# Banded attention's value product on 64-column stationary tiles, three products in the same rows of PSUM

## The chip, the cores and the metric

The kernel runs on one core of one Trainium2 chip. The metric is the device time of one launch in microseconds (us), lower is better. The core has five engines with a queue of instructions each, worked off in order: TensorE (PE, matmuls; the load of a stationary tile is PEld), VectorE (DVE), ScalarE (ACT), GpSimd (POOL) and SyncE (SP), which here issues most of the transfers between memory and SBUF. Matmuls write to PSUM, which has eight banks of 512 float32 columns on 128 rows; ACT and DVE read it.

## The reference

Two layers of a decoder trunk on 1024 positions of width 1024. In each layer one projection feeds three groups of heads (an mLSTM, a sliding-window attention, a differential attention), their outputs are concatenated and multiplied by `w_out`, normalised and added to `x`; a squared-ReLU MLP of width 4096 follows. The part that the change touches is the sliding-window attention: 8 query heads of 64 columns, which share 2 key-value heads, four each; the window is 128 keys, so that a block of 128 queries sees its own block of keys and the one before it.

```python
s = jnp.einsum('bnqhgd,bnkhd->bnhgqk', qb, kb).astype(jnp.float32) * (D ** -0.5)
...
s = jnp.where(valid[None, :, None, None], s, -jnp.inf)
sink = sinks.astype(jnp.float32).reshape(Hkv, G)[None, None, :, :, None]
mx = jnp.maximum(jnp.max(s, axis=-1), sink)
e = jnp.exp(s - mx[..., None])
denom = jnp.sum(e, axis=-1) + jnp.exp(sink - mx)
p = e / denom[..., None]
o = jnp.einsum('bnhgqk,bnkhd->bnqhgd', p.astype(v.dtype), vb)
```

The last line is the value product. Everything is float32.

## The kernel before, in words

**Precision.** The matmuls take a float32 format that keeps fewer bits. So the operands are split: `split(hi, lo, src)` (lines 92 to 94) lets ACT cast the source to that format (`hi`) and DVE subtract `hi` from the source (`lo`). A product is then the sum of hi x hi, hi x lo and lo x hi: three matmuls that accumulate in one PSUM tile. In the value products of the two attentions it is done in another way: the stationary tile holds the high half of the values in columns 0 to 63 and the low half in columns 64 to 127, so that one matmul gives both products, in rows 0 to 63 and 64 to 127 of PSUM, and two matmuls (with the high and with the low half of the probabilities) give all four. The two halves of the rows are then to be added.

**The stages of a layer.** Projections (PSUM tiles `pt`, `pg`, `pn`), the differential attention (`sp`, `trd`, `pv`), then the banded attention and the mLSTM side by side, then the output projection in two groups of four tiles of `w_out` (`po`), the first with the differential attention and key-value head 0, the second with key-value head 1 and the mLSTM; behind each row tile of the second group come the norm, the residual and the transposes (`post_mix`). Then the MLP (`pu` and `pd`).

**The banded attention** goes over 2 key-value heads and 8 query blocks, 16 steps in a layer. `swa1` makes the scores `ss` of four heads, masks them, and leaves the normalised probabilities in `es` (pool `pt`, two buffers). `swa2` belongs to the step before: for each of its one or two key blocks it transposes the four heads' probabilities into a PSUM tile `trs` (tag `as`, two banks, which the scores use too), splits it into one of two SBUF tiles `sb_pt`, and multiplies with the values `v6s` into `pvs`, which has one bank. Behind the last key block ACT copies rows 64 to 127 to `ys`, DVE adds them to rows 0 to 63 into `yy` (two buffers; one addition for each half of the heads, the second of which moves to rows 64 to 127), and `split` writes `yy` into the tile `mxl` that the output projection reads. `mxl` lies in pool `e`, which has four buffers: one per row tile and output group, free again when that group's matmuls on this row tile are done.

**What sets the order.** The program is traced in Python; a planner gives each engine's queue its order by priorities (`ahead` raises them) and by when operands and buffers are free in its own estimate of time. `run` draws the steps of the banded attention (17, raised by 300 in layer 0 and by 200 in layer 1) and of the mLSTM (10) in turn. Buffers of one tag are handed out as they become free. The scores' operands `kk` and `qq` fill the four buffers of pool `ws`; the second output group's first two weight tiles take the same four (line 999). The mLSTM loads its rows anew in each step (`mb<-m_rows`, lines 748 and 755).

Lines of the profile around the change: 612 (`ss`), 641 (`trs`), 93 and 94 (`split`), 646 (`pvs`), 649 (`ys`), 654 (`yy`), 849 (`po`), 855 and 857 (its evacuation), 153 (`rs`, the norms' reciprocal roots on POOL).

Of the kernel before, what the change touches and what calls it, by code (L numbers as in the profile page):

```python
# [17 lines left out]
P = 128  # L18
# [16 lines left out]
def hybrid_kernel(ctx: ExitStack, tc: tile.TileContext, x_in, w_t, w_g, w_v, w_out, w_up, w_down,  # L35
                  pb, cv, gains, g_mlp, rope_t, masks, out):
    nc = tc.nc
# [9 lines left out]
    def pool(tag, bufs, space=None):  # L47
        kw = {} if space is None else {"space": space}
        pools[tag] = ctx.enter_context(tc.tile_pool(name="p_" + tag, bufs=bufs, **kw))
# [8 lines left out]
    pool("ev", 6)  # L58
    pool("raw", 2)
    pool("od", 3)  # L60
    pool("ys", 1)
    pool("mo", 1)
    pool("yy", 2)
    pool("mm", 2, PSUM)
    pool("ad", 2, PSUM)
    pool("as", 2, PSUM)
# [6 lines left out]
    def new(tag, shape, name, dt=F32):  # L73
        return pools[tag].tile(list(shape), dt, name=name, tag=tag)
# [10 lines left out]
    def PS(tag, name):  # L85
        return new(tag, (P, 512), name)
# [5 lines left out]
    def split(hi, lo, src):  # L92
        nc.scalar.copy(hi, src)  # L93
        nc.vector.tensor_sub(lo, src, hi.bitcast(F32))  # L94
# [123 lines left out]
    for l in range(DEPTH):  # L218
# [129 lines left out]
        v6s = sb[:, 0:2048].rearrange("p (t c) -> p t c", t=NT)  # L348
# [216 lines left out]
        def mx_tile(grp, t):  # L565
            if (grp, t) not in mxs:
                mxs[grp, t] = new("e", (P, 2, 4, P), "mxl", F32R)
            return mxs[grp, t]
# [64 lines left out]
        def swa2(kv, i):  # L633
            e = sst[kv, i]
            pv = PS("pvs", "pvs")
            nb_ = 1 if i == 0 else 2
            for j in range(nb_):
                kb = i if i == 0 else i - 1 + j
                tr = PS("as", "trs")
                for hh in range(4):  # L640
                    nc.tensor.transpose(tr[:, hh * P:(hh + 1) * P], e[:, hh, j * P:(j + 1) * P], ident)
                pt = sb_pt[ptn[0] % 2]
                ptn[0] += 1
                split(pt[:, 0], pt[:, 1], tr)
                for s in range(2):
                    nc.tensor.matmul(pv, lhsT=v6s[:, kb, kv * P:(kv + 1) * P], rhs=pt[:, s],  # L646
                                     start=j == 0 and s == 0, stop=j == nb_ - 1 and s == 1)
            y = new("ys", (64, 512), "ys")
            nc.scalar.copy(y, pv[64:128])
            y4 = y.rearrange("p (a b c) -> p a b c", a=2, b=2)  # L650
            p4 = pv.rearrange("p (a b c) -> p a b c", a=2, b=2)
            yy = new("yy", (P, 2, P), "yy")
            for b in range(2):
                nc.vector.tensor_add(yy[b * 64:(b + 1) * 64], y4[:, :, b, :], p4[0:64, :, b, :])
            mx = mx_tile(kv, i)
            k0 = 2 if kv == 0 else 0
            split(mx[:, 0, k0:k0 + 2], mx[:, 1, k0:k0 + 2], yy)


        zprev = {}  # L660
# [224 lines left out]
        def e_swa():  # L885
            ssteps = [(kv, i) for kv in range(2) for i in range(NT)]
            for i in range(len(ssteps) + 1):
                if i < len(ssteps):
                    swa1(*ssteps[i])
                if i >= 1:  # L890
                    swa2(*ssteps[i - 1])
                yield
# [310 lines left out]
```

## Time and profile before

| | |
|---|---|
| time, median of 3 runs | 2480.98 us (2479.06 to 2483.18) |
| profiled execution, its own time | 2487.86 us |
| its span | 2486.1 us |
| mean granted clock of TensorE | 0.984 |
| busy: PE, PEld, DVE, ACT, POOL | 2380.3, 1977.1, 1456.5, 1074.4, 91.3 us |
| matmuls | 11556 |
| moved by DMA | 227.42 MB, mean 91 GB/s |

A row of a group names the line, the engine, the operation, what is written and what is read (by the program's names), the shape, the count, then the busy time in us and the mean length of one in ns, and the idle time of the engine just before them with what ended it. Matmuls overlap: the length of one is longer than the distance between two in a row. The chain is followed back from the last instruction, at each step to what released it. `PEclk` and the clock in a table of stretches are the share of full speed that was granted to TensorE.

### The profile page before, as it was taken

How to read it: one execution, taken by the hardware profiler on the slowest of the kernel's cores; microseconds unless marked ns; L12 is line 12 of the kernel's file. 1: busy time of each engine (PE TensorE's matmuls, PEld its weight loads, DVE VectorE, ACT ScalarE, POOL GpSimd, SP SyncE). 2: the span in 40 equal slices, each digit the busy share in tenths (PEclk: the TensorE clock that was granted, in tenths of full speed). 3: DMA queues.
4: the chain of work that ended last, by engine and by line, in shares of the span. 5: the costliest groups of instructions: out<-in, count | busy, mean ns of one | idle time of the engine just before them, and what ended most of it. 6: DMA issues, size and time to landing. Idle time of an engine off the chain costs nothing.

```text
span 2486.1 us, 32491 instructions
## 1 busy us (share of the span) xinstructions
PE 2380.3 (96%) x11556; PEld 1977.1 (80%) x11556; DVE 1456.5 (59%) x3604; ACT 1074.4 (43%) x2657; POOL 91.3 (4%) x174
## 2 busy tenths in 40 slices
PE   8999979789999999999999999888899999999998
PEld 7889867668888888888778889766688888888887
DVE  5798978674334433543686988777734334434436
ACT  4356867464312321331434757765644123212312
POOL 0000000010000000000000001000100000000000
PEclk9999999899999999999999999989999999999999
DMA  4554253432101201210552453433322012101204
GB/s 166 176 181 133 72 155 98 104 121 68 51 26 60 68 29 40 68 51 26 169 179 86 137 169 109 135 101 96 119 68 68 26 43 68 51 26 60 68 26 161
DMA packets 146866, 227.42 MB, mean 91 GB/s; under 512 B 23376, under 2 KB 61456, under 8 KB 146704
## 3 DMA queue, kind: packets, MB, share of 16 engines
q1 hardware_dynamic: 144544, 221.70, 28.3%
q10 hardware_dynamic: 2160, 3.65, 0.4%
q8 instruction: 91, 1.49, 0.2%
q14 instruction: 71, 0.58, 0.1%
HBM read 179.09 MB, written 46.20 MB: 91 GB/s over the span
## 4 chain that ended last, share of the span: by engine, by line
PE 78%; DVE 8%; DMA 5%; ACT 4%; issue 2%; POOL 2%; SPq 0%; POOLq 0%; DVEq 0%; ACTq 0%
PE pu L1013 26%; PE pd L1058 26%; PE pt L286 9%; PE po L849 3%; PE pn L358 3%; PE pg L358 2%; POOL rs L153 2%; DMA mb<-m_rows 2%; PE pv L530 2%; PE sp L495 1%; PE trd L522 1%; DMA mxl<-mix_d 1%; PE ss L612 1%; ACT junk L159 1%; PE pvs L646 1%
## 5 line engine op out<-in xcount | busy, mean ns | idle before, releaser
L1013 PE MATMUL pu<-h2T,wu 128*128 128x512 f32 x3072 | 704.7, 391 | 0.8 <-ACT h2T L93 0.8
L1013 PEld LDWEIGHTS pu<-h2T,wu 128*128 128x128 f32 x3072 | 577.8, 188 | 122.4 <-DVE h2T L94 1.3
L1058 PE MATMUL pd<-wdh,u 128*128 128x512 f32 x2048 | 635.2, 390 | 1.6 <-DVE acm L1069 1.6
L1058 PEld LDWEIGHTS pd<-wdh,u 128*128 128x128 f32 x2048 | 384.7, 188 | 81.6 <-DVE acm L1069 2.0
L1058 PE MATMUL pd<-wdl,u 128*128 128x512 f32 x1024 | 399.0, 390 | 0.0
L1069 DVE TENSOR_TENSOR acm<-acm,pd 128x512 f32<-128x512 f32 x224 | 153.1, 686 | 309.2 <-PE pd L1058 309.2
L1016 ACT ACTIVATE r<-pu 128x512 f32<-128x512 f32 x128 | 75.2, 588 | 537.0 <-PE pu L1013 536.2
L286 PE MATMUL pt<-hT,wt 128*128 128x512 f32 x832 | 279.5, 401 | 2.0 <-DVE lamp L228 1.5
L116 ACT ACTIVATE wu<-rw,gk 128x128 fp32r<-128x128 f32 x512 | 160.3, 390 | 185.9 <-PE pu L1013 133.8
L117 DVE SCALAR_TENSOR_TENSOR wu<-rw,gk,wu 128x128 fp32r<-128x128 f32 x512 | 154.0, 350 | 140.1 <-ACT wu L116 140.1
L1058 PEld LDWEIGHTS pd<-wdl,u 128*128 128x128 f32 x1024 | 192.5, 188 | 39.9
L1019 DVE TENSOR_TENSOR r<-r 128x512 f32<-128x512 f32 x128 | 88.3, 690 | 221.5 <-ACT u L1018 221.5
L286 PEld LDWEIGHTS pt<-hT,wt 128*128 128x128 f32 x832 | 155.5, 190 | 31.0 <-issue 1.9
L286 PE MATMUL pt<-lT,wt 128*128 128x512 f32 x416 | 166.0, 399 | 0.0
L153 POOL TENSOR_TENSOR rs<-ms,mhalf 128x1 f32<-128x1 f32 (+2 forms) x112 | 79.4, 713 | 2284.3 <-DVE ms L151 2215.9
L94 DVE TENSOR_TENSOR wdl<-rw,wdh 128x512 fp32r<-128x512 f32 x128 | 88.5, 692 | 106.4 <-ACT wdh L93 106.3
L849 PE MATMUL po<-woh,mxl 128*128 128x512 f32 x384 | 134.8, 410 | 8.2 <-DVE acc L857 6.6
L93 ACT CAST wdh<-rw 128x512 fp32r<-128x512 f32 x128 | 79.3, 619 | 131.6 <-DMA rw<-in_w_down_dram 131.5
L501 ACT ACTIVATE e<-e,nb 128x256 f32<-128x256 f32 (+7 forms) x128 | 99.4, 777 | 37.8 <-DVE nb L498 37.3
L358 PE MATMUL pn<-wv,hT 128*128 128x256 f32 x512 | 106.5, 289 | 0.2 <-ACT mv L708 0.2
L849 PEld LDWEIGHTS po<-woh,mxl 128*128 128x128 f32 x384 | 73.3, 194 | 22.9 <-DVE acc L857 7.9
L1020 DVE TENSOR_TENSOR u<-r,u 128x512 fp32r<-128x512 f32 x128 | 88.5, 691 | 4.0
(225 smaller groups left out, 3329.2 us busy)
## 6 DMA issues: line engine op xcount, KB each, us to landing
rw<-in_w_up_dram SPq DMA_DIRECT2D x128, 256.0 KB, 2.9
rw<-in_w_down_dram SPq DMA_DIRECT2D x128, 256.0 KB, 2.8
rw<-in_w_t_dram SPq DMA_DIRECT2D x52, 256.0 KB, 3.0
tab<-in_rope_dram SPq DMA_DIRECT2D x20, 512.0 KB, 4.4
xt<-in_x_dram SPq DMA_DIRECT2D x16, 512.0 KB, 4.2
d_rope<-rot SPq DMA_DIRECT2D x32, 256.0 KB, 3.2
s_ropeq<-rot SPq DMA_DIRECT2D x32, 256.0 KB, 2.7
qq<-s_ropeq SPq DMA_DIRECT2D x16, 512.0 KB, 5.0
```

Of the source, the lines that this page charges most:

```text
L94: nc.vector.tensor_sub(lo, src, hi.bitcast(F32))
L116: nc.scalar.activation(hi[:, cs], rj, AF.Copy, scale=g)
L117: nc.vector.scalar_tensor_tensor(out=lo[:, cs], in0=rj, scalar=g, in1=hi[:, cs].bitcast(F32), op0=ALU.mult, op1=ALU.subtract)
L153: nc.gpsimd.tensor_tensor(out=rs, in0=ms, in1=mhalf[:, 0:n], op=ALU.pow)
L286: nc.tensor.matmul(q, lhsT=a, rhs=b, start=n == 0, stop=n == 23)
L358: nc.tensor.matmul(q[:, 0:n], lhsT=a, rhs=b, start=i == 0, stop=i == 23)
L501: nc.scalar.activation(e[:, 0:L], e[:, 0:L], AF.Exp, bias=nb[:, nch - 1:nch], scale=-1.0, accum_out=den[:, m:m + 1])
L849: nc.tensor.matmul(q, lhsT=mx[:, a, k], rhs=wo[k][b][:, n * 512:(n + 1) * 512], start=i == 0, stop=i == 3 * nk - 1)
L1013: nc.tensor.matmul(q, lhsT=w[:, a, kc], rhs=h2[b + half][:, :, kc], start=n == 0, stop=n == 23)
L1020: nc.vector.tensor_sub(us[1][:, hs], r, us[0][:, hs].bitcast(F32))
L1058: nc.tensor.matmul(q, lhsT=U[f][a][:, t * P:(t + 1) * P], rhs=D[f][b][:, n * 512:(n + 1) * 512], start=i == 0, stop=i == 3 * nf - 1)
L1069: nc.vector.tensor_add(a, a, q)
```

## The change

The value product of the banded attention takes the high and the low half of the values as two stationary tiles of 64 columns. Three products (high x high, high x low, low x high; low x low is left out) accumulate in rows 0 to 63 of `pvs`. `ys`, `yy`, the copy and the additions go, and with them the two pools; the split into `mxl` reads `pvs` itself, once for each half of the heads, 64 rows at a time.

```diff
@@ -58,9 +58,7 @@
     pool("ev", 6)
     pool("raw", 2)
     pool("od", 3)
-    pool("ys", 1)
     pool("mo", 1)
-    pool("yy", 2)
     pool("mm", 2, PSUM)
     pool("ad", 2, PSUM)
     pool("as", 2, PSUM)
@@ -642,19 +640,16 @@
                 pt = sb_pt[ptn[0] % 2]
                 ptn[0] += 1
                 split(pt[:, 0], pt[:, 1], tr)
-                for s in range(2):
-                    nc.tensor.matmul(pv, lhsT=v6s[:, kb, kv * P:(kv + 1) * P], rhs=pt[:, s],
-                                     start=j == 0 and s == 0, stop=j == nb_ - 1 and s == 1)
-            y = new("ys", (64, 512), "ys")
-            nc.scalar.copy(y, pv[64:128])
-            y4 = y.rearrange("p (a b c) -> p a b c", a=2, b=2)
-            p4 = pv.rearrange("p (a b c) -> p a b c", a=2, b=2)
-            yy = new("yy", (P, 2, P), "yy")
-            for b in range(2):
-                nc.vector.tensor_add(yy[b * 64:(b + 1) * 64], y4[:, :, b, :], p4[0:64, :, b, :])
+                for n, (a, b) in enumerate(((0, 0), (0, 1), (1, 0))):
+                    c0 = kv * P + a * 64
+                    nc.tensor.matmul(pv[0:64], lhsT=v6s[:, kb, c0:c0 + 64], rhs=pt[:, b],
+                                     start=j == 0 and n == 0, stop=j == nb_ - 1 and n == 2)
+            p4 = pv[0:64].rearrange("p (a b c) -> p a b c", a=2, b=2)
             mx = mx_tile(kv, i)
             k0 = 2 if kv == 0 else 0
-            split(mx[:, 0, k0:k0 + 2], mx[:, 1, k0:k0 + 2], yy)
+            for b in range(2):
+                rr = slice(b * 64, (b + 1) * 64)
+                split(mx[rr, 0, k0:k0 + 2], mx[rr, 1, k0:k0 + 2], p4[:, :, b, :])
 
 
         zprev = {}
```

## The prediction

> **What bounds the kernel now.** I read the page first: its busy shares and the chain that ended last.
>
> ```profile
> span 2486.1 us, 32491 instructions
> ...
> PE 2380.3 (96%) x11556; PEld 1977.1 (80%) x11556; DVE 1456.5 (59%) x3604; ACT 1074.4 (43%) x2657; POOL 91.3 (4%) x174
> ...
> PE 78%; DVE 8%; DMA 5%; ACT 4%; issue 2%; POOL 2%; SPq 0%; POOLq 0%; DVEq 0%; ACTq 0%
> ```
>
> TensorE (PE) is the bound of the whole, so an edit that gives it work and relieves the others starts with a debt. But the shares are a mean over stages. The banded attention runs from about 262 to 510 us in layer 0 and from 1500 to 1745 us in layer 1. So next I took the busy time in these two stretches, first of everything, then of the instructions that touch the value product's PSUM tile `pvs` (columns: stretch, length, PE, PEld, DVE, ACT, POOL or, in the second pair, PE, PEld, DVE, ACT; then granted clock, DMA share, GB/s).
>
> ```profile
> 262.00:510.00 248.00, 214.83 (x1101) 171.95 (x1100) 193.41 (x630) 164.71 (x467) 14.71 (x29) 0.94 0.36 105
> 1500.00:1745.00 245.00, 217.60 (x1276) 184.55 (x1276) 189.38 (x654) 160.48 (x477) 16.58 (x31) 0.94 0.37 105
> ```
> ```profile
> 262.00:510.00 248.00, 24.93 (x60) 12.17 (x60) 13.17 (x32) 9.32 (x16) 0.94 0.36 105
> 1500.00:1745.00 245.00, 24.33 (x60) 11.99 (x60) 13.17 (x32) 9.32 (x16) 0.94 0.37 105
> ```
>
> Here PE is busy 87 to 89% of the time, DVE 77 to 78%, ACT 66%. No engine is full: PE idles 33 and 27 us. What ends the waits is seen in the chain of the same stretches, by line, and in its longest pieces.
>
> ```profile
> by line: PE pt L286 13.9%; PE po L849 13.4%; DMA mb<-m_rows 9.8%; PE pvs L646 5.1%; PE ss L612 4.9%; DMA mxl<-mix_d 4.2%; PE trs L641 3.4%; DMA rw<-in_w_up_dram 3.2%; issue 2.8%; POOL rs L153 2.3%; ACT es L621 2.3%; PE spm L763 2.2%; DMA rw
> ...
> 391.68 7.50 DMA mb<-m_rows
> 433.89 7.66 DMA mb<-m_rows
> 458.17 9.14 DMA mb<-m_rows
> ```
> ```profile
> by line: PE po L849 12.1%; PE pn L358 9.6%; DMA mb<-m_rows 6.4%; DMA mxl<-mix_d 6.4%; PE ss L612 5.5%; PE pvs L646 4.9%; issue 4.9%; PE spm L763 4.0%; PE trs L641 3.8%; PE pv L530 3.3%; DMA rw<-in_w_up_dram 3.2%; POOL rs L153 2.8%; PE trd L
> ```
>
> The chain runs over PE much of the time and stops for loads of the mLSTM's rows, 7.5 to 9.1 us each. The value product (`pvs`) itself lies on it for 5.1% of 248 and 4.9% of 245 us, 12.6 + 12.0 = 24.6 us.
>
> **The change, part by part.** The groups of instructions by line and shape (busy us, mean ns of one, idle before):
>
> ```profile
> L1013 PE MATMUL pu<-h2T,wu 128*128 128x512 f32 x3072 | 704.7, 391 | 0.8 <-ACT h2T L93 0.8
> ```
> ```profile
> L522 PE MATMUL trd<-mk,e 128*128 128x128 f32 x288 | 56.3, 281 | 3.2 <-DVE on L549 2.4 <-DVE e L508 0.4 <-ACT oo L559 0.2
> L646 PE MATMUL pvs<-sb 128*128 128x512 f32 x120 | 49.3, 462 | 8.3 <-ACT sb L93 6.4 <-DVE yy L654 1.6
> ```
> ```profile
> L557 PE MATMUL tb<-mk,on 128*64 128x128 f32 x64 | 13.0, 277 | 1.1 <-DVE on L549 1.0
> ```
> ```profile
> L649 ACT COPY ys<-pvs 64x512 f32<-64x512 f32 x32 | 18.6, 583 | 15.5 <-PE pvs L646 15.0
> L93 ACT CAST mxl<-yy 128x256 fp32r<-128x256 f32 x32 | 12.9, 404 | 6.7 <-PE po L849 4.5 <-DVE yy L654 2.2
> ```
> ```profile
> L559 ACT COPY oo<-tb 64x256 f32<-64x256 f32 x32 | 11.6, 361 | 0.7 <-PE tb L557 0.7
> ```
> ```profile
> L93 ACT CAST v6d<-pg 128x256 fp32r<-128x256 f32 x16 | 6.0, 376 | 2.8 <-DVE sb L94 2.8
> ```
> ```profile
> L654 DVE TENSOR_TENSOR yy<-ys,pvs 64x256 f32<-64x256 f32 x64 | 26.3, 412 | 6.8 <-ACT ys L649 6.1
> L94 DVE TENSOR_TENSOR mxl<-yy,mxl 128x256 fp32r<-128x256 f32 x32 | 13.4, 418 | 0.3 <-ACT mxl L93 0.3
> ```
>
> 1. *Matmuls.* There are 60 pairs of a key block and a key-value head (15 per head and layer); each goes from two matmuls to three, 120 to 180. All still stream 512 columns, so halving the stationary columns saves nothing of the streaming. One such matmul in a dense row costs 704.7 / 3072 = 0.229 us, 60 of them 13.8 us, or 14.6 us at this stage's granted clock of 0.94. Bounds: nothing, where PE would have waited for a row load anyway, and 60 x 49.3/120 = 24.7 us by what the present ones occupy with their waits. The weight loads get shorter, but overlap matmuls already. Of the present 49.3 us, 24.6 lie on the chain, one half; I take the same half of 14.6: **+7.3 us**.
>
> 2. *ScalarE.* 32 copies to `ys` (18.6) and 32 casts of `yy` (12.9) go; 64 casts of 64x256 out of PSUM come, nearest row the copy of `tb`, 361 ns: 23.1. Net -8.4 us.
>
> 3. *VectorE.* 64 additions (26.3) and 32 subtractions (13.4) go; 64 subtractions of 64x256 with one operand in PSUM come, the form of the additions, 412 ns: 26.4. Net -13.3 us. What of 2 and 3 shortens the path: on the page 8% of the span is DVE's part of the chain, 199 of its 1456.5 busy us, 14%; ACT's 4% is 99 of 1074.4, 9%. So 13.3 x 0.14 + 8.4 x 0.09 = **-2.6 us**. Bounds: 0 and -21.7, every microsecond of both.
>
> 4. *Latency of one evacuation.* Now 0.58, two additions of 0.41, 0.40 and 0.42, 2.2 us. The new one is two casts and two subtractions on one PSUM bank. The row of `v6d` shows ACT waiting for a DVE subtraction that reads the same bank (other columns), so I expect them one after the other: 2 x (0.36 + 0.41) = 1.5 us. The 0.7 us gained per block hides behind other work: `mxl` from `yy` was awaited for 0.3 us by DVE and by nothing longer. The bank is held 1.5 us, against 1.4 now. 0 to the sum.
>
> 5. *Removal of `yy`.* This is the part that could turn. Two `yy` buffers and `ys` stand today between `pvs` (one bank) and the four slots of pool `e` that hold `mxl`. The rows of the second head in layer 0:
>
> ```profile
> 434.34 0.42 DVE L94 TENSOR_TENSOR mxl<-yy,mxl 128x256 fp32r<-128x256 f32 x1
> ```
> ```profile
> 435.02 0.84 DVE L654 TENSOR_TENSOR yy<-ys,pvs 64x256 f32<-64x256 f32 x2
> ```
> ```profile
> 436.24 0.63 PE L646 MATMUL pvs<-sb 128*128 128x512 f32 x2
> ```
> ```profile
> 462.05 0.42 DVE L94 TENSOR_TENSOR mxl<-yy,mxl 128x256 fp32r<-128x256 f32 x1
> ```
> ```profile
> 462.70 0.83 DVE L654 TENSOR_TENSOR yy<-ys,pvs 64x256 f32<-64x256 f32 x2
> ```
>
> A slot of `mxl` comes free, `yy` empties into it, the next `pvs` empties into `yy`, then the next product starts: already today the products follow the slots, three blocks ahead. Without `yy` they follow one block behind. Two links hang on that: the last transposes free `es`, the last scores `ss` free the `ws` slots, and only then can the second output group's weights be split into those slots. Layer 0, then layer 1 (the last scores; in layer 0 the weight load right behind them; the last copy of the first output group; the last weight split; the mLSTM's last `rs`, merged with that of the first row norm, which starts the closing series):
>
> ```profile
> 447.45 1.05 PE L612 MATMUL ss<-kk,qq 128*128 128x256 f32 x4
> ```
> ```profile
> 449.12 0.95 SPq L109 DMA_DIRECT2D rw<-in_w_out_dram  x2
> ```
> ```profile
> 460.28 0.59 ACT L855 COPY acc<-po 128x512 f32<-128x512 f32 x1 [0.22 <-PE po L849]
> ```
> ```profile
> 471.89 0.69 DVE L94 TENSOR_TENSOR wol<-rw,woh 128x512 fp32r<-128x512 f32 x1 [0.24 <-ACT woh L93]
> ```
> ```profile
> 511.62 1.53 POOL L153 TENSOR_TENSOR rs<-ms,mhalf 128x4 f32<-128x4 f32 x2 [4.09 <-DVE ms L151]
> ```
> ```profile
> 1689.53 0.64 PE L612 MATMUL ss<-kk,qq 128*128 128x256 f32 x4
> ```
> ```profile
> 1701.80 0.59 ACT L855 COPY acc<-po 128x512 f32<-128x512 f32 x1 [0.32 <-PE po L849]
> ```
> ```profile
> 1710.22 0.69 DVE L94 TENSOR_TENSOR wol<-rw,woh 128x512 fp32r<-128x512 f32 x1 [0.22 <-ACT woh L93]
> ```
> ```profile
> 1744.07 1.53 POOL L153 TENSOR_TENSOR rs<-ms,mhalf 128x4 f32<-128x4 f32 x2 [4.14 <-DVE ms L151]
> ```
>
> In the new order the last scores come after the first output group (460.9), an evacuation (1.5), a product of three matmuls (0.9), a cast and a subtraction of 512 columns (0.6 + 0.7, as `ys` and `wol`) and two rounds of scores (1.05 each): 467, in place of 448.5, and the last weight is split 24.1 us behind that as now, at 491 in place of 472.6: 18 us late, and about as much in layer 1. But the first four row tiles of that group take 96 x 0.229 = 22 us of PE and only the first is needed when the closing series starts at 513, behind the mLSTM. So 491 is early enough, and 1729 still is for 1746. I take **0**; the bound is 18 us per layer, +36.
>
> The sum: 7.3 - 2.6 = +4.7 us on the profiled execution's own 2487.86 us (span 2486.1): 2492.6. That execution was 6.9 us above the median of the runs, 2480.98; on that scale **2486**.
>
> One rule speaks against the change. The Trainium skill, TensorEngine Tiling (Array Packing), Key Properties, says that changing the tiling mode drains TensorE, and lists 128 rows by 64 columns as a mode of its own. By that rule each of 60 groups would drain twice. In this trace `tb`, with 64 stationary columns between neighbours of 128, takes 277 ns against 281 for `trd` with 128, so nothing of a drain is seen; by the rule the sum would be some +24, and it is a rival below.
>
> **The rivals.**
> A, the forecast (38%): half of the new matmul time is exposed, 2486, own range 2478 to 2494.
>
> B (20%): PE's extra 14.6 us fall into the 33 + 27 us it idles while row loads fly, and the relief was off the path too. For it: three row loads alone hold the chain 24 us in layer 0. Against it: half of `pvs` is on the chain. 2481, no change.
>
> C (25%), faster: after a load lands, the chain runs through the backlog in ACT's and DVE's queues, and each block now leaves 21.7 / 32 = 0.7 us less there. For it: a stall in those in-order queues stops PE too. Against it: the chain's 14% and 9%. With half the relief on the path and the matmuls under the loads, -11: 2470.
>
> D (14%), slower: the late slots of part 5 are exposed. It decides as soon as the second group's first tile comes later than the mLSTM's end, which needs only that the mLSTM, freed of competing blocks, ends earlier, or that the weight loads queue behind others on SP. With half the bound, +18 on top of the 4.7: 2504.
>
> E (3%), slower: PE runs empty where the number of stationary columns changes, 0.39 - 0.23 = 0.16 us (the 391 ns of one matmul against 0.229 in a row) at both ends of 60 groups, +19 on top of 4.7: 2505.
>
> **How the numbers follow.** What this kernel's measurement can tell from no change is about 0.2%, 5 us. The order of all queues is drawn anew by the planner, which smears every case by several us. A gives slower 0.20, same 0.15, faster 0.03; B 0.05, 0.10, 0.05; C faster 0.20, same 0.05; D and E slower 0.17. Together faster 0.28, same 0.30, slower 0.42. The range reaches from C to D and E: 2466 to 2508.
>
> **What would show it.** Step 1: 180 `pvs` matmuls on 128x64 stationary tiles, 0.23 apart in a row; PE busy up by 10 to 15 us. A drain would show as a gap of some 0.16 us on both sides of them. Steps 2 and 3: no `ys` or `yy`, 64 casts near 360 ns and 64 subtractions near 412 ns out of `pvs`, ACT and DVE busy down 8 and 13. Step 4: cast and subtraction of one block never overlapping. Step 5: products of the second head starting right behind an `mxl` subtraction, last `ss` near 467 instead of 448, and the mLSTM's last `rs` still ahead of the closing series. I am wrong if the closing series starts earlier than 511 us by more than 5 (then C), or waits for `po` instead of `rs` (then D).

## The result, and the profile after it

The changed kernel takes 2520.82 us (median; 2516.48 to 2522.76), the kernel before 2482.08 (2479.06 to 2483.25) beside it: ratio 1.0156, 95% interval 1.0137 to 1.0174. It is 38.7 us slower. The forecast was 2486 with a range to 2508; the time lies above the range. One execution in all that follows, of 2974.9 us with three products and four `yy`, ran at a clock of 0.745 in place of 0.99; it is left out of that kernel's ratio but counts in its median of 2466.4, which would be 2464.9 without it.

The page of the profiled execution of the kernel after: span, busy times, and the shares of the chain that ended last.

```profile
span 2520.9 us, 32554 instructions
...
PE 2395.4 (95%) x11616; PEld 1978.8 (78%) x11616; DVE 1448.5 (57%) x3572; ACT 1072.8 (43%) x2657; POOL 94.0 (4%) x174
...
PE 77%; DVE 7%; DMA 7%; ACT 5%; issue 2%; POOL 2%; SPq 0%; DVEq 0%; POOLq 0%; ACTq 0%
```

PE has 15.1 us more work (2395.4 for 2380.3), DVE 8.0 and ACT 1.6 less. That work was priced about right. But the span grew by 34.8 us, more than twice the added work, and on the chain the shares that grew are DMA's, 7% for 5%, and ScalarE's, 5% for 4%. The same two stretches as before (columns: stretch, length, PE, PEld, DVE, ACT, POOL, clock, DMA share, GB/s), and then a pair from the banded attention's start to the MLP's first matmul, in the kernel after and in the kernel before:

```profile
262.00:510.00 248.00, 204.80 (x1028) 159.00 (x1027) 176.06 (x582) 151.70 (x436) 16.05 (x30) 0.91 0.35 98
1500.00:1745.00 245.00, 210.18 (x1314) 176.44 (x1314) 182.12 (x637) 155.79 (x469) 18.22 (x33) 0.96 0.38 108
262.00:567.00 305.00, 255.85 (x1266) 198.44 (x1265) 220.89 (x666) 189.91 (x511) 25.12 (x43) 0.92 0.36 107
```
```profile
262.00:539.00 277.00, 241.17 (x1229) 192.76 (x1228) 217.89 (x671) 184.56 (x501) 20.59 (x39) 0.94 0.37 109
```

In layer 0 all three engines do less in the same 248 us: PE 10 us, DVE 17, ACT 13. Nobody is overloaded; everybody waits. Up to the MLP, PE is idle 305 - 255.9 = 49 us where it was idle 277 - 241.2 = 36. The ground is lost early: from 380 to 460 us PE is busy 61.0 us for 72.4 before, and the granted clock is 0.92 up to 425 us and 0.85 behind it, for 1.00 and 0.95; from 460 to 493 us PE does more than before (28.4 for 22.7 us). The MLP's first matmul and, behind the layer's last one, the first of the next layer, after and then before:

```profile
566.74 1.07 PE L1008 MATMUL pu<-h2T,wu 128*128 128x512 f32 x4
...
1275.53 0.39 PE L284 MATMUL pt<-hT,wt 128*128 128x512 f32 x1
...
1812.81 1.07 PE L1008 MATMUL pu<-h2T,wu 128*128 128x512 f32 x4
```
```profile
539.34 0.84 PE L1013 MATMUL pu<-h2T,wu 128*128 128x512 f32 x3
...
1256.51 0.39 PE L286 MATMUL pt<-hT,wt 128*128 128x512 f32 x1
...
1771.80 1.52 PE L1013 MATMUL pu<-h2T,wu 128*128 128x512 f32 x6
```

These rows split the 34.8 us of span. Attention and mixing of layer 0: +27.4 (566.74 - 539.34). The MLP of layer 0: 708.8 for 717.2, -8.4. Attention and mixing of layer 1: 537.3 for 515.3, +22.0. The MLP of layer 1, to the end of the span: 708.1 for 714.3, -6.2. Before, the MLP's first matmuls ran beside the end of the closing series (see the last section), so the net of a layer, 19.0 and 15.8 us, says more than 27.4 and 22.0.

The value product's own instructions after (duration min, median, max), and what ended the idle time ahead of them:

```profile
L645 PEld LDWEIGHTS pvs<-sb x180: 132/134/231, 299.9 to 1802.5; 128*64 128x64 f32 x180
L645 PE MATMUL pvs<-sb x180: 387/396/686, 300.1 to 1802.5; 128*64 128x512 f32 x180
L91 ACT CAST mxl<-pvs x64: 347/364/372, 309.2 to 1804.6; 64x256 fp32r<-64x256 f32 x64
L92 DVE TENSOR_TENSOR mxl<-pvs,mxl x64: 384/417/419, 310.5 to 1805.0; 64x256 fp32r<-64x256 f32 x64
...
  DVE mxl L92: 34.4, 25
```

The durations are near those of the prediction (cast 0.364 for 0.361, subtraction 0.417 for 0.412). New is the last row: 34.4 us in which an engine stood still until a subtraction into `mxl` was done, where before the largest such row was a cast of `sb` with 18.9. One such place in the timeline of layer 0 (start, length, engine, line, operation; in brackets the idle time ahead and its releaser):

```profile
426.46 0.90 PE L645 MATMUL pvs<-sb 128*64 128x512 f32 x3
...
448.11 0.36 ACT L91 CAST mxl<-pvs 64x256 fp32r<-64x256 f32 x1 [0.22 <-DVE mxl L92]
452.19 0.69 DVE L753 TENSOR_TENSOR mb<-mb,mk 128x512 f32<-128x512 f32 x1 [4.03 <-DMA mb<-m_rows]
452.91 0.42 DVE L92 TENSOR_TENSOR mxl<-pvs,mxl 64x256 fp32r<-64x256 f32 x1
453.39 2.22 PE L645 MATMUL pvs<-sb 128*64 128x512 f32 x6 [3.67 <-DVE mxl L92]
454.48 0.56 ACT L91 CAST sb<-trs 128x512 fp32r<-128x512 f32 x1
457.43 0.78 PE L610 MATMUL ss<-kk,qq 128*128 128x256 f32 x4
...
492.30 0.74 PE L610 MATMUL ss<-kk,qq 128*128 128x256 f32 x4 [0.25 <-DVE sb L92]
493.03 1.29 DVE L92 TENSOR_TENSOR wol<-rw,woh 128x512 fp32r<-128x512 f32 x2
...
506.71 0.69 DVE L92 TENSOR_TENSOR wol<-rw,woh 128x512 fp32r<-128x512 f32 x1 [0.67 <-ACT woh L91]
```

The product that ends at 427.4 stays in its bank until 447.1, when its first cast starts: 19.7 us. That is the wait for a slot. The first casts of the second head's first four blocks, at 447.06, 466.48, 477.02 and 486.03, each start 0.8 us behind the copy that ends a row tile of the first output group (446.28, 465.70, 476.23, 485.26), and a slot is free when that group is done with its row tile. Not all of the hold is the slot's: the second subtraction, at 452.91, stands in VectorE's queue behind an operation that waits 4.03 us for the mLSTM's rows.

The PSUM bank is given back at 453.3, the next product starts, only then do the waiting transposes leave PSUM (`sb`), and only then come the next scores. So the chain of the prediction's part 5 is there, but later than it said: the last scores end at 493.0 (448.5 before, 467 predicted), the last weight is split at 507.4 (472.6 and 491). SP's queue tells the same. Its longest wait, in the stretch 340 to 520 us (total, times, longest), is a load of output weights that stands until a split has taken its buffer's content:

```profile
SPq L107 <- DVE wol L92: 38.8, 6, 33.2
```

SP issues no load for 33 us, and the rows of `x` for the closing series are queued behind it. Meanwhile the mLSTM, which competes for PE, was done sooner, and the closing series waits for `po`. The mLSTM's last `rs` and last copy `mo`, the series' first `rs`, and its first updates and loads of `xt`; then the mLSTM's last copy before:

```profile
468.60 1.01 POOL L151 TENSOR_TENSOR rs<-ms,mhalf 128x4 f32<-128x4 f32 x1 [2.87 <-DVE ms L149]
472.06 0.40 ACT L813 COPY mo<-tbm 128x256 f32<-128x256 f32 x1
511.09 0.56 POOL L151 TENSOR_TENSOR rs<-ms,mhalf 128x1 f32<-128x1 f32 x1 [41.48 <-DVE ms L149]
511.68 1.29 DVE L990 SCALAR_TENSOR_TENSOR xt<-ag,rs,xt 128x1024 f32<-128x1024 f32 x1 [0.41 <-POOL rs L151]
516.59 0.33 SPq L986 DMA_DIRECT2D xt<-in_x_dram  x1
520.27 1.28 DVE L990 SCALAR_TENSOR_TENSOR xt<-ag,rs,xt 128x1024 f32<-128x1024 f32 x1 [0.91 <-DMA xt<-in_x_dram]
530.63 1.28 DVE L990 SCALAR_TENSOR_TENSOR xt<-ag,rs,xt 128x1024 f32<-128x1024 f32 x1
```
```profile
518.10 0.35 ACT L818 COPY mo<-tbm 128x256 f32<-128x256 f32 x1
```

Before, the mLSTM's last `rs` and the series' first ran back to back at 511.6; now 41 us lie between them. The series starts no later than it did, at 511, but its first two steps take 8.6 and 10.4 us where they took 4.4 and 6.2, and it takes 59 us to its last row tile for 39 before (first to last update of `xt`: 511.7 to 570.6, before 513.2 to 552.6). The last products of the banded attention, done by 484 us before, now fall into it: the last one starts at 556.4. The block ahead of it, which is evacuated from 536.4 to 554.1, stands in front of the series' longest step, 14.3 us (549.9 to 564.2).

### The profile page after: what moved, and what is told of

The parts are those of the page before. It is cut to its first block, busy times and chain, and to the rows that moved or that the text cites. A ratio compares the mean times of both kernels' runs of the same rounds, so it can differ in the third digit from the quotient of the medians.

```text
span 2520.9 us, 32554 instructions
## 1 busy us (share of the span) xinstructions
PE 2395.4 (95%) x11616; PEld 1978.8 (78%) x11616; DVE 1448.5 (57%) x3572; ACT 1072.8 (43%) x2657; POOL 94.0 (4%) x174
## 4 chain that ended last, share of the span: by engine, by line
PE 77%; DVE 7%; DMA 7%; ACT 5%; issue 2%; POOL 2%; SPq 0%; DVEq 0%; POOLq 0%; ACTq 0%
PE pu L1008 26%; PE pd L1053 25%; PE pt L284 8%; PE po L844 3%; PE pg L356 3%; PE pn L356 3%; DMA mb<-m_rows 3%; DMA mxl<-mix_d 2%; PE pv L528 1%; POOL rs L151 1%; PE sp L493 1%; ACT junk L157 1%; PE pvs L645 1%; PE trd L520 1%; PE tr L171 1%
## 5 line engine op out<-in xcount | busy, mean ns | idle before, releaser
L844 PE MATMUL po<-woh,mxl 128*128 128x512 f32 x384 | 142.4, 427 | 9.9 <-ACT woh L91 9.2
L844 PEld LDWEIGHTS po<-woh,mxl 128*128 128x128 f32 x384 | 75.8, 200 | 27.9 <-ACT woh L91 13.8
```

Of the source, the lines that this page charges most:

```text
L844: nc.tensor.matmul(q, lhsT=mx[:, a, k], rhs=wo[k][b][:, n * 512:(n + 1) * 512], start=i == 0, stop=i == 3 * nk - 1)
```

## The experiments

Four theories stood. *Lost buffers* (T1): without `yy` the product's one PSUM bank waits for a slot of `mxl`. *Matmul work* (T2): 60 more matmuls on the bound engine. *A drain* at the 64-column tiles (T3). *Chance* (T4): the planner draws a new order. In the excerpts of code, `...` stands for further lines of the same place. Each time is a median, each ratio is to the kernel before run beside it on the same chip (2479 to 2482 us), with its 95% interval.

**1. The three products, with `yy` back.** The bank is emptied by two VectorE copies into `yy`, which is split as before:

```
+    pool("yy", 2)
...
+            yy = new("yy", (P, 2, P), "yy")
+            for b in range(2):
+                nc.vector.tensor_copy(yy[b * 64:(b + 1) * 64], p4[:, :, b, :])
...
-            for b in range(2):
-                rr = slice(b * 64, (b + 1) * 64)
-                split(mx[rr, 0, k0:k0 + 2], mx[rr, 1, k0:k0 + 2], p4[:, :, b, :])
+            split(mx[:, 0, k0:k0 + 2], mx[:, 1, k0:k0 + 2], yy)
```

> The three 64-column products of the kernel after, but the value tile is evacuated as before into a staging tile yy of two buffers (two VectorE copies of 64x256 out of PSUM, then one cast and one subtraction of 128x256). Lost buffers (T1): the slack between the product's PSUM bank and the four mxl slots is back, last ss of layer 0 near 448 us again, time 2480 to 2492 (the 60 added matmuls, up to 14 us, less 18.6 us of ScalarE copies). Matmul work or a drain at the 64-column tiles (T2, T3): the products are those of the kernel after, so the time stays at 2515 to 2525. New order by chance (T4): anywhere between.

> As the run with three products and two yy buffers, but with four of them, the same SBUF as before (the 2 KB of ys goes into them). Lost buffers (T1): the products may run five blocks ahead of the mxl slots instead of three, last ss of layer 0 ahead of 448; time equal to or up to 10 us under that run with two, if what is gained there isn't only waiting elsewhere. T2, T3: 2515 to 2525.

> Three products with eight yy buffers, so that a whole half-sequence of blocks can wait in front of mxl. Lost buffers, more slack: last ss of layer 0 as with four (440), since es and the row loads now set it, and the time within 4 us of the four-buffer kernel, 2462 to 2469. If slack were still short at four: 2456 to 2462.

> Three products, the short evacuation (two VectorE copies of 64x256), and one yy buffer; two gave 2472.6, four 2466.4, and without a buffer the same evacuation straight into the mxl slot 2521.8. If the loss is the step from one buffer to none: 2455 to 2480. If one buffer leaves half of it here: 2490 to 2505.

One buffer: 2488.0 us (ratio 1.0023, 1.0010 to 1.0036). Two: 2472.6 (0.9963, 0.9948 to 0.9978). Four: 2466.4 (0.9941, 0.9921 to 0.9960). Eight: 2466.4 (0.9948, 0.9930 to 0.9966). The 60 matmuls and the 64-column tiles are in all of them, so T2 and T3 don't carry the loss. Against two buffers the kernel after loses 48 us. Two buffers came out below the range that T1 had given, and one between its two ranges. The value product's matmuls with four buffers:

```profile
L646 PE MATMUL pvs<-sb x180: 387/393/775, 301.4 to 1680.3; 128*64 128x512 f32 x180
```

The last product now starts at 1680 in layer 1; it was 1802.5 in the kernel after. What the first buffers buy is a lead, not a shorter wait: with one, two and four buffers the second head's products of layer 0 wait 104.2, 79.8 and 31.2 us in sum for their evacuation to start, in the kernel after 70.0 (worked out from the instructions on `pvs`), while the last scores end at 478, 451 and 441 us, after at 493.

**2. The old products, with fewer or more `yy`.** Without any, the additions write into the slot of `mxl` itself:

```
-    pool("yy", 2)
...
-            yy = new("yy", (P, 2, P), "yy")
...
-                nc.vector.tensor_add(yy[b * 64:(b + 1) * 64], y4[:, :, b, :], p4[0:64, :, b, :])
...
-            split(mx[:, 0, k0:k0 + 2], mx[:, 1, k0:k0 + 2], yy)
+            raw = mx[:, 1, k0:k0 + 2]
...
+                nc.vector.tensor_add(raw[b * 64:(b + 1) * 64], y4[:, :, b, :], p4[0:64, :, b, :])
+            split(mx[:, 0, k0:k0 + 2], raw, raw.bitcast(F32))
```

> The two 128-column products of the kernel before with the ys copy, but without yy: the two additions write straight into the low half of the mxl slot, which is then cast and subtracted in place. The sum is rounded to the matmul's format before it is split, so the low half of the attention's value is zero; every instruction of before is still there. Lost buffers (T1): the product's bank is given back only when an mxl slot is free, so the time is 2505 to 2521, last ss of layer 0 near 485 to 493. Matmul work or drain (T2, T3): no 64-column matmul and none added, 2480 to 2485. New order by chance (T4): anywhere between.

> The kernel before with one yy buffer in place of two. Shortage of buffers: a step between none (2517.2) and two (2481), 2488 to 2508, last ss of layer 0 between 448 and 483. An order of the queues that turns only when there is no buffer at all: 2478 to 2486.

> The kernel before with four yy buffers in place of two. Lost buffers: if slack still pays beyond two, as from 2472.6 to 2466.4 us in the three-product kernels, 3 to 8 us faster, 2472 to 2478. If the gain of the three-product kernels with yy comes from the shorter evacuation (the ys copy gone) alone, no change, 2478 to 2484.

None: 2517.2 us (1.0146, 1.0123 to 1.0169). One: 2464.0 (0.9943, 0.9923 to 0.9963). Two is the kernel before. Four: 2476.3 (0.9987, 0.9976 to 0.9998). The first of these has every matmul and every evacuating instruction of before, and is 36 us slower all the same. The value product's rows without `yy`, and its last scores in layer 0:

```profile
L645 PE MATMUL pvs<-sb x120: 387/396/777, 301.6 to 1791.3; 128*128 128x512 f32 x120
L655 DVE TENSOR_TENSOR mxl<-ys,pvs x64: 401/414/416, 312.0 to 1793.3; 64x256 fp32r<-64x256 f32 x64
```
```profile
481.91 0.72 PE L611 MATMUL ss<-kk,qq 128*128 128x256 f32 x4
```

So the loss is the missing buffer. One buffer missed what was expected of it by a wide margin: not a step between none and two, but 15 us better than two (2464.0 for 2479.3 beside it). With the same instructions, one, two and four buffers give 2464, 2480 and 2476, in no order. That is T4 in a measured size: kernels with the same instructions, which differ only in the number of buffers and in the order that the planner makes of it, lie up to 15 us apart, more than the "several us" of the prediction. The size of the loss is known no better than that: with the old products none costs 53, 36 and 41 us against one, two and four buffers, with the new ones 33, 48, 54 and 54 against one, two, four and eight.

**3. Straight into `mxl`, by one engine.** The kernel after empties the bank by turns of ScalarE and VectorE. Here VectorE alone copies into the slot's low half (`raw`, as in 2) and the split runs in SBUF:

```
...
-                split(mx[rr, 0, k0:k0 + 2], mx[rr, 1, k0:k0 + 2], p4[:, :, b, :])
+                nc.vector.tensor_copy(raw[b * 64:(b + 1) * 64], p4[:, :, b, :])
+            split(mx[:, 0, k0:k0 + 2], raw, raw.bitcast(F32))
```

> Three products and no yy, as in the kernel after, but the bank is emptied by VectorE alone: two copies of 64x256 into the low half of the mxl slot, then cast and subtraction in place out of SBUF (the copies round to the matmul's format, so the low half of the attention's value is zero). Missing buffer: the bank still waits for an mxl slot, 2505 to 2520. Two-engine evacuation: 2472 to 2490, as with yy of two buffers (2472.6).

2521.8 us (1.0163, 1.0144 to 1.0182), the time of the kernel after. From a block's first evacuating instruction to the end of its last, the median over 32 blocks is 0.85 us here and 3.42 in the kernel after (worked out from the instructions that read `pvs`; 2.31 before). The way out of the bank doesn't matter here as long as there is nothing to empty it into.

**4. Slots of `e` in place of `yy`.** One line is changed in the kernel after, `pool("e", 4)` to 5 and 6:

> The kernel after, with the 4 KB per partition that ys and yy gave up spent on a fifth slot of the pool e (mxl, xt, e). Lost buffers (T1): one slot of slack is back where three half-size buffers were lost; a third to all of the 38 us, 2483 to 2508, last ss of layer 0 between 448 and 480. T2, T3: 2515 to 2521, since the matmuls are the same. New order by chance (T4): anywhere.

> The kernel after, with two more slots in pool e (six). In the run with five the first evacuation of the second head came 20 us sooner (427 for 447), but the rest hung on the output projection of the first head's tiles, which was itself later, and the time stayed. Lost buffers: with six, three of the second head's blocks are evacuated before that projection ends; last ss of layer 0 at 460 to 485 and 2490 to 2515. If a slot is no substitute for yy because the planner spends it on earlier tiles: 2515 to 2525 again. T2, T3: 2515 to 2525.

Five: 2522.3 us (1.0170, 1.0150 to 1.0190), nothing gained. Six: 2495.3 (1.0061, 1.0043 to 1.0079), 25 us back. The expectation for five failed. Its trace shows the second head's first two evacuations, and the first group's copy that the second waited for; the kernel after beside it:

```profile
427.23 0.37 ACT L91 CAST mxl<-pvs 64x256 fp32r<-64x256 f32 x1
...
463.96 0.59 ACT L850 COPY acc<-po 128x512 f32<-128x512 f32 x1
464.75 0.36 ACT L91 CAST mxl<-pvs 64x256 fp32r<-64x256 f32 x1
```
```profile
446.28 0.59 ACT L850 COPY acc<-po 128x512 f32<-128x512 f32 x1 [1.97 <-PE po L844]
447.06 0.36 ACT L91 CAST mxl<-pvs 64x256 fp32r<-64x256 f32 x1
...
466.48 0.36 ACT L91 CAST mxl<-pvs 64x256 fp32r<-64x256 f32 x1
```

With a fifth slot the first evacuation came 20 us earlier. The second waits for the slot that the fifth tile of the first output group frees; in the kernel after it was the first evacuation that started behind that tile's copy, at 446.3. With five slots the copy came at 464.0, and the lead was gone. A slot of `e` is freed by the output projection, which runs behind; a buffer of `yy` is freed by a cast and a subtraction, which need a slot themselves. Two `yy` cost a quarter of the SBUF of two slots and did more; why is not shown.

**5. The links behind the bank.** Three kernels cut the chain of part 5 at one place each, `yy` still gone: four slots for `es` (`pool("pt", 4)`); own slots for the rows of `x` in the closing series; four slots for `es` and the second head's scores in another PSUM pair.

```
+    pool("xx", 2)
...
-            xt = new("pt", (P, DM), "xt2")
+            xt = new("xx", (P, DM), "xt2")
```
```
-    pool("pt", 2)
+    pool("pt", 4)
...
-                sp = PS("as", "ss")
+                sp = PS("ad" if kv else "as", "ss")
```

> The kernel after with four slots for es (and the xt rows) in place of two, yy still gone. Lost buffers by the chain mxl slot, pvs bank, es slot, ss, ws slot, weight load: the link at es is cut, last ss of layer 0 back to 440 to 465, the output weights' loads no longer keep SP's queue shut for 33 us, and the closing series starts near 500; the evacuations of the last four blocks still wait for mxl. 2485 to 2505. If only the number of mxl slots counts: 2515 to 2525.

> The kernel after with the xt rows of the closing series in a pool of their own, of two slots, instead of sharing the two of es. The last link alone: in the trace after, the second and third row tiles of the series wait for a load that had one slot, since es held the other until 531 us. If that stretches the series (59 us for 39): 8 to 15 us back per layer, 2495 to 2510, with last ss still near 490. If the series is stretched by late mxl evacuations on PE alone: 2515 to 2525.

> The kernel after with four es slots, and the scores of the second head in the PSUM pair ad (which the mLSTM uses too) instead of as. In the run with four es slots alone, the transposes of the third block sat in both banks of as from 434 to 455 us, waiting for a buffer behind the blocked product, and the next scores came at 459. If those banks are the link: last ss of layer 0 at 455 to 480 for 495, SP's queue open sooner, 2495 to 2515. If the link is elsewhere: last ss stays at 490 to 495 and 2520 to 2535.

Four `es`: 2529.5 us (1.0196, 1.0178 to 1.0214), and the last scores stayed at 494.8. The prediction's link, "the last transposes free `es`", is not what held them. The timeline of that run:

```profile
433.85 0.63 PE L639 MATMUL trs<-mk,es 128*128 128x128 f32 x4
434.55 0.62 PE L639 MATMUL trs<-mk,es 128*128 128x128 f32 x4
454.88 2.82 PE L645 MATMUL pvs<-sb 128*64 128x512 f32 x6 [4.28 <-DVE mxl L92]
456.45 0.59 ACT L91 CAST sb<-trs 128x512 fp32r<-128x512 f32 x1 [0.42 <-PE pvs L645]
457.74 0.59 ACT L91 CAST sb<-trs 128x512 fp32r<-128x512 f32 x1 [0.69 <-PE pvs L645]
458.66 0.60 PE L610 MATMUL ss<-kk,qq 128*128 128x256 f32 x3
```

Two transposed blocks sit in PSUM from 435 to 456, in the pair of banks that scores and transposes share; the buffers they are cast into are those of the product that waits for its bank. Moving the scores to another pair gave 2516.0 (1.0135, 1.0116 to 1.0155), 13.5 us less, but the last scores still came at 487.9, which the expectation had at 455 to 480, and the mLSTM uses that pair; 13.5 us is also no more than a new order alone can make. So this link isn't settled. Own slots for `x`: 2515.6 (1.0145, 1.0131 to 1.0159); the first row tiles of the closing series are 7.3 and 7.5 us apart for 8.6 and 10.4, but the interval overlaps that of the kernel after. Of the three only this one came out in an expected range, that of little gain. No single link behind the bank is worth the loss.

**6. What the products and the evacuation cost by themselves.** The low product issued twice (with two and with four `yy`); three 64-column products with the whole evacuation of before; two 128-column products with the short evacuation, which leaves rows 64 to 127 out:

```
-                for s in range(2):
+                for n, s in enumerate((0, 1, 1)):
```
```
+            y = new("ys", (64, 512), "ys")
+            nc.scalar.copy(y, pv[0:64])
...
+                nc.vector.tensor_tensor(out=yy[b * 64:(b + 1) * 64], in0=y4[:, :, b, :], in1=p4[:, :, b, :], op=ALU.max)
```
```
-            nc.scalar.copy(y, pv[64:128])
...
-                nc.vector.tensor_add(yy[b * 64:(b + 1) * 64], y4[:, :, b, :], p4[0:64, :, b, :])
+                nc.vector.tensor_copy(yy[b * 64:(b + 1) * 64], p4[0:64, :, b, :])
```

> The kernel before, with the product of the low weights issued twice for each key block and head (so the low half counts twice): 60 more 128-column matmuls of 512 columns and nothing else. Matmul work exposed by half, as the forecast had it: +7.3 us, 2486 to 2492. Matmul work hidden in PE's idle time: 2478 to 2484. All of it exposed: +14.6, 2495. Lost buffers: says nothing, since yy and ys stay.

> The kernel before with the product of the low weights doubled (60 more matmuls, the low half counted twice) and four yy buffers. If the matmuls cost 23 us because the products then run into the same shortage of buffers: 2480 to 2490, and against the kernel before with four buffers (2476.3) 4 to 14. If they cost it as work on PE: 2497 to 2503.

> Three 64-column products, with the whole evacuation of before put back: ys copied by ScalarE, two VectorE operations of 64x256 from ys and PSUM into yy (two buffers; a maximum of the same numbers stands for the addition), cast, subtraction. Against the kernel before this is the change of the matmuls alone, against the kernel with the short evacuation (2472.6) that of the evacuation alone, against the doubled 128-column product (2502.8) that of 64 for 128 stationary columns. If 60 more matmuls cost 23 us whatever their width: 2498 to 2508, and the short evacuation is worth some 30. If 64 columns are cheaper to issue than 128: 2478 to 2492. Forecast of the prediction: +7.3, 2487.

> Two 128-column products as before, with the short evacuation: the ys copy is left out and two copies take rows 0 to 63 alone into yy (two buffers), so the product with the low weights is not added to the output. If the shorter hold of the PSUM bank (0.84 for 1.41 us) is worth some 30 us: 2445 to 2460. If it is worth what the prediction gave ScalarE and VectorE, 2 to 3 us: 2475 to 2483.

| products | evacuation | `yy` | us | ratio (95%) |
|---|---|---|---|---|
| 2 x 128 columns | `ys`, two additions | 2 | 2480 | 1 |
| 2 x 128 | two copies | 2 | 2465.1 | 0.9942 (0.9929 to 0.9955) |
| 3 x 64 | `ys`, two operations | 2 | 2505.3 | 1.0104 (1.0089 to 1.0119) |
| 3 x 64 | two copies | 2 | 2472.6 | 0.9963 (0.9948 to 0.9978) |
| 3 x 128 | `ys`, two additions | 2 | 2502.8 | 1.0096 (1.0078 to 1.0115) |
| 3 x 128 | `ys`, two additions | 4 | 2499.4 | 1.0069 (1.0048 to 1.0090) |

Three readings. First, 64 or 128 stationary columns make no difference (2505.3 and 2502.8, intervals that overlap). The trace of the kernel after shows no drain either: from the start of a 512-column matmul on 128 stationary columns to the start of a product on 64 right behind it the median is 0.234 us (26 places), on the way back 0.235 (59 places), where the kernel before has 0.236 and 0.277 at its 128-column products. T3 falls. Second, 60 more matmuls cost some 7.5 us with the short evacuation (5 by the ratios, whose intervals just overlap) and 23 to 25 with the long one; their work is 13.8. Third, the `ys` copy that the change took away was worth 15 us with the old products and 33 with the new, not part of 2.6. The doubled product and the short evacuation of the old products both lie outside their expected ranges. The terms don't add; each leans on the other. Four `yy` did not bring the 23 us down to the expected 4 to 14, so that is not the shortage of buffers. What the engines waited for in the stretch 395 to 450 us with the doubled product and two `yy` (total, times, longest), and that stretch's busy times and clock there and in the kernel before:

```profile
ACT mb L756 <- DMA mb<-m_rows: 14.3, 2, 7.5
DVE mxl L94 <- ACT mxl L93: 12.2, 2, 7.3
PE spm L763 <- DVE mb L795: 12.1, 2, 7.1
```
```profile
395.00:450.00 55.00, 42.74 (x237) 35.81 (x236) 36.35 (x145) 30.50 (x97) 2.01 (x2) 0.88 0.26 74
```
```profile
395.00:450.00 55.00, 47.49 (x259) 38.02 (x259) 43.34 (x171) 37.68 (x116) 2.13 (x2) 0.97 0.34 81
```

PE's queue stands 12 us for the rows of the mLSTM, by way of three queues: ScalarE waits for the rows, a cast into `mxl` stands behind that, VectorE waits for the cast, and the update of the mLSTM's state that PE needs stands behind VectorE's wait. The kernel before does not have this wait there, and the granted clock is 0.88 for 0.97. Why the planner's order meets these loads so badly with the longer products is open.

**7. Both at once.** Three products, short evacuation, four `yy`, and five slots in `e`:

> Three products, short evacuation, four yy buffers, and a fifth slot in pool e. If slots still pay: 2455 to 2463. If the four buffers have taken all there was (last ss at 440 with four and with eight): 2462 to 2470.

2500.8 us (1.0077, 1.0062 to 1.0093): above both expected ranges and 34 us slower than the same kernel with four slots, although the last scores come at 445.6 in layer 0, earlier than before. In the stretch 340 to 440 us PE is busy 81.6 us, with four slots 91.3:

```profile
340.00:440.00 100.00, 81.63 (x417) 62.95 (x416) 75.91 (x277) 58.90 (x176) 2.02 (x2) 0.87 0.36 108
```
```profile
340.00:440.00 100.00, 91.25 (x504) 72.22 (x505) 86.26 (x326) 68.88 (x219) 3.02 (x3) 0.97 0.45 122
```

A resource added where there was no shortage can cost as much as the one taken away. What in the new order did it is not shown. So T4 can make as much as 34 us, and no single pair of kernels refutes it as the cause of the loss. All of them together speak against it: the seven kernels without `yy` and with four or five slots of `e` lie between 2516 and 2530 us, the twelve with at least one `yy` between 2464 and 2505.

The start of layer 0's last value product, beside the time, over these kernels:

| kernel | last product, us | time, us |
|---|---|---|
| before | 483 | 2480 |
| old products, `yy` 1 / 4 | 489 / 459 | 2464 / 2476 |
| old products, short evacuation | 477 | 2465 |
| three products, `yy` 1 / 2 / 4 / 8 | 533 / 518 / 461 / 457 | 2488 / 2473 / 2466 / 2466 |
| no `yy`: after / old products / one engine | 556 / 540 / 554 | 2521 / 2517 / 2522 |
| no `yy`: five / six slots of `e` | 545 / 519 | 2522 / 2495 |
| no `yy`: 4 `es` / own `x` / other PSUM | 551 / 544 / 542 | 2530 / 2516 / 2516 |
| 3 x 64, long / 3 x 128, long / with `yy` 4 | 532 / 538 / 491 | 2505 / 2503 / 2499 |
| three products, `yy` 4, `e` 5 | 461 | 2501 |

With a last product behind 530 us, inside the closing series, no kernel is below 2488. An early one is not enough, as the last two rows show (491 us and 2499, 461 and 2501); that it is needed is a reading of the table, not a test.

## Why the prediction was wrong, step by step

*Matmuls, +7.3.* The work was right: PE's busy time grew by 15.1 where 10 to 15 were named, and a matmul's median is 396 ns for 402. The exposure is some 7.5 us with the short evacuation, which agrees with the forecast within a noise of some 5 us; beside the `ys` copy it is 23 to 25, the upper bound of the step. In the kernel after it can't be told from the rest.

*ScalarE and VectorE, -2.6.* Too small. The work of the group came down as reckoned: 64 casts of 364 ns and 64 subtractions of 417 in place of 31.5 and 39.7 us, -8.2 and -13.0. (The engines' whole busy time fell only by 1.6 and 8.0.) But the price was taken from the engines' share of the chain, which says nothing of how long the bank is held. Leaving out `ys` with `yy` kept is worth 15 to 33 us in the runs. The change could not collect that.

*Latency of one evacuation, 0.* The cast and the subtraction do run one after the other, as said. But 1.5 us was the sum of four durations, and the 1.4 of before that of three; in the traces the medians are 3.42 and 2.31 us and the longest after 17.7, since each turn between two in-order queues can meet a wait there, as at 448 to 453 us above. By the run with one engine this made no difference to the time, because the slot was the limit.

*Removal of `yy`, 0.* This is the step that failed: "So 491 is early enough, and 1729 still is for 1746. I take 0; the bound is 18 us per layer, +36." Against two buffers the runs put the price at 36 us with the old products and 48 to 49 with the new (2521 and 2522 against 2472.6). Three things in it were wrong. The last scores came at 493, not 467: the estimate left the end of the first output group at 460.9, and that group ended at 485.8. From there the reckoning nearly held, 7.3 us to the last scores for 5.8. Why the group itself came 25 us later is shown only in part: in the time up to 460 us PE stands for the cast of `sb` (7.9 us from 380 to 425), for a VectorE step of the mLSTM and for the product's bank (4.7 and 3.7 from 425 to 460). The closing series was compared with an mLSTM that keeps its place, and the mLSTM moved forward by 46 us (`mo`'s last copy at 472.1 for 518.1 before), so that the series' first step waited for `po`, 41 us behind the mLSTM's last `rs`. And the third effect was not seen at all: not only the weights are late, the products of the last three blocks themselves fall into the closing series.

*The rivals.* D had the mechanism and its condition, "which needs only that the mLSTM, freed of competing blocks, ends earlier, or that the weight loads queue behind others on SP": the first happened, and on SP it was a weight load that waited for its own buffer and held up the others. Its price of half the bound was too low. It had 14%. E falls: three 64-column products in place of three of 128 columns change nothing (2505.3, 2502.8), and its gap of 0.16 us is not there: 0.234 and 0.235 us from start to start, where it would ask for 0.39. The Trainium skill, TensorEngine Tiling (Array Packing), Key Properties, says that changing the tiling mode drains TensorE; no drain shows at these products, and whether 64 stationary columns change the mode at all, no run here can tell. A, B and C are out by their time, though A's +7.3 for the matmuls came true where buffers were there.

*The range.* It added D's half bound to the forecast and stopped at 2508. The text's own bound, +36 on 2486, would have held the time, but by luck: it had the last weight 18 us late in layer 0, and it was 35 us late (507.4 for 472.6). "Smears every case by several us" was too small as well: up to 15 us between kernels with the same instructions, and 34 us for one slot more.

## What to carry to other kernels

Here a small staging buffer between PSUM and a slow consumer is what let the products run ahead on a single PSUM bank; before it is removed as a copy too many, ask how long each slot behind it is held, and by whom. A shorter way out of the bank pays only where there is something to empty it into: two copies by one engine into two buffers of 1 KB per partition beat a direct split that saved them. When a stall moves, don't keep the rest of the picture still: the work that competed with the stalled part ran ahead here, and the cover it gave was gone.

The three products are not bad in themselves: with the short evacuation and four buffers in the SBUF of before they take 2466.4 us. The old products with a single `yy` take 2464.0, so the gain over the kernel before can't be put down to the products.

## What was not expected of the chip

The 64-column weight load takes 134 ns for 188 of the 128-column one, but the time of the kernel doesn't show it. In stretches with more waits the granted clock is lower: 0.88 in the one with 12 us of waits above, where it was 0.97. In the kernel after, 512-column `po` matmuls at 445 us, behind a wait of 4 us at 437 to 441, start 0.43 us apart (445.18, 445.61, 446.04); with two `yy`, without that wait, they start 0.23 apart at the same time (445.17, 445.40, 445.63). So a stall can be paid a second time in slower matmuls. And a late attention gives part back: the MLP that follows took 708.8 and 708.1 us for 717.2 and 714.3. Before, its first matmuls (539.3) ran beside the end of the closing series (552.6), after hardly at all (566.7 and 570.6); that this overlap is the cause is a reading, not a test.
